# A two-layer decoder trunk: conv taps of one FFN quarter issued a unit later, and two block subtractions written as one

## The chip, the core and the metric

The kernel runs on one core of a Trainium2 chip. The core has five engines that run their own instruction streams in program order and wait for each other through semaphores: PE (TensorE, matmuls; its weight loads are listed as PEld), DVE (VectorE), ACT (ScalarE), POOL (GpSimd) and SP (SyncE, which here only issues DMAs). The metric is the time of one execution on the device in microseconds; less is better. "us" below is microseconds.

## What is computed

Layer 0 is a pooling mixer and a conv FFN, layer 1 an attention over one shared K/V and a conv FFN, each followed by a residual sum and a layer norm. All is in float32, 256 tokens by 2048 features. What the change touches is the conv FFN (hidden width 5504 for the gate and as many for the value):

```python
def conv_ffn(h, w_up, conv_w, conv_b, w_down):
    S = h.shape[1]
    u = h @ w_up
    up = jnp.pad(u, ((0, 0), (CONV_WIDTH - 1, 0), (0, 0)))
    c = conv_b + up[:, 0:S] * conv_w[0]
    for j in range(1, CONV_WIDTH):
        c = c + up[:, j:j + S] * conv_w[j]
    gate, val = jnp.split(c, 2, axis=-1)
    return (jax.nn.silu(gate) * val) @ w_down
```

## The kernel before

**Units.** All matrix products with weights are cut into units, one for each block of up to 512 rows by 512 columns of a weight matrix. `units` lists them in the order in which PE takes them; each entry has the weight block, a function that issues the matmuls, a `post` for the last unit of a group, and, for some blocks of the down-projection, a kind "a" or "b". `run_units` (L126) walks through the list. For unit i it calls `ahead(i)`, which issues loads for up to five units further on and splits for up to three units further on; then it issues the unit's matmuls; then every entry of `pending` that is due; then the `post`. `later(n, fn)` puts a function on `pending` for n units on, and `later(0, fn)` calls it at once. So the list of units and the calls of `later` fix the program order on every engine by hand.

**Splits.** A weight block comes by DMA (SP, L72) into one of three `raw` buffers. ACT rounds it to a high part `wh` (L82) and DVE subtracts to get the low part `wl` (L83); each has four buffers. A product of two such numbers takes three matmuls: high by high, low by high, high by low. A load waits until the raw buffer of three loads ago was split, and a split waits until PE has left the buffer of four units ago.

**Blocks with seven products.** For many blocks of the down-projection the 2 x 2 block product is done with seven products in place of eight (Strassen's scheme in Winograd's form). There the weight block is split twice: kind "a" takes three of the four quadrants as they are, kind "b" the sums of quadrants. `split_sums` (L90) makes both. With r11 and r12 the left and right halves of the upper rows (`B1`) and r21, r22 those of the lower rows (`B2`), kind "a" casts the left half and r22 on ACT (L103), then issues on DVE the difference r12 - r11 (L104), the two low parts (L106), and three differences, each written over its input (L107 to L109). Kind "b", one unit later, casts the right half and then the left half on ACT (L96) and subtracts for the low parts (L97). There are 46 such pairs. The sums on the activation side are made in `left_sums` (L625); its third sum (L647) is the one that multiplies the left upper quadrant of kind "b".

**The FFN.** `ffn(lay)` (L548) takes the hidden width in quarters q0 to q10 of 512 (q10 has 384). `up(q, ...)` puts four units for the gate half and four for the value half; between them stand groups of the down-projection of earlier quarters. A group is one block of 512 output columns (`c`). When the value half of a quarter has run, `val_post` calls `val_chain` (L665): `evac` copies the sums out of the accumulators (L577 on ACT, L578 on DVE), then `conv` issues the three taps (L586 and L591 on ACT, L592 on DVE), `valued` multiplies with the gate (L670), and `three` splits the product into `gq[q]`, tile `g` (L287 on ACT, L283 on DVE), which the down-projection reads as left operand. When `conv` is issued is set by the last line of `val_chain` through `done`, `after` and `at`: `done` has an entry for q4 and q7 alone; for all others the default counts, which is the unit that has just run, plus 0 or 1. With `quick` (q10 alone) the second and third tap are issued together with the first, otherwise one and two units later. `three` is issued at least one unit after `valued`.

**The last stretch.** In layer 1 the value half of q10 is the last of the up-projection. Behind it stand the groups of the last part of the down-projection over q8, q9 and q10. Blocks of q9 have seven products in column blocks 0 and 2. `turns` (L452) puts the first unit of column block 1 ahead of the last one of column block 0, so that the order is: q8 of block 0, q9 of block 0 (a, then b), q8 of block 1, q10 of block 0, q9 of block 1, q10 of block 1, and so on. The matmuls of q8 and q10 are those of `go_t` (L235 to L237), those of q9 with seven products L224 to L226. The first unit that reads q10's `g` is the fifth behind the up-projection.

Of the kernel before, what the change touches and what calls it, by code (L numbers as in the profile page):

```python
# [13 lines left out]
OP = mybir.AluOpType  # L14
# [4 lines left out]
P = 128  # L19
NQ = 4  # L20
FF = 5504
NF = FF // P
# [10 lines left out]
def trunk(ctx: ExitStack, tc: tile.TileContext, x, pool_w_in, pool_w_grp, pool_scale, pool_w_out,  # L33
# [3 lines left out]
    V, A, PE = nc.vector, nc.scalar, nc.tensor  # L37
# [15 lines left out]
    state = {"loaded": 0, "split": 0, "done": 0}  # L53
# [34 lines left out]
    B1, B2, N1, N2 = slice(0, 2), slice(2, 4), slice(0, 256), slice(256, 512)  # L88

    def split_sums(i, kind):  # L90
        h = wh[i] = wp.tile([P, 4, 512], F32R, name=f"wh{i}", tag="wh")
        l = wl[i] = wp.tile([P, 4, 512], F32R, name=f"wl{i}", tag="wl")
        if kind == "b":
            r = raw.pop(i - 1)
            for n in (N2, N1):
                A.copy(h[:, :, n], r[:, :, n])  # L96
                V.tensor_tensor(l[:, :, n], r[:, :, n], h[:, :, n].bitcast(F32), OP.subtract)  # L97
            return
        r = raw[i]
        r11, r12, r21, r22 = r[:, B1, N1], r[:, B1, N2], r[:, B2, N1], r[:, B2, N2]  # L100
        parts = [(slice(0, 4), N1), (B2, N2)]
        for k, n in parts:
            A.copy(h[:, k, n], r[:, k, n])  # L103
        V.tensor_tensor(r12, r12, r11, OP.subtract)  # L104
        for k, n in parts:
            V.tensor_tensor(l[:, k, n], r[:, k, n], h[:, k, n].bitcast(F32), OP.subtract)  # L106
        V.tensor_tensor(r22, r22, r12, OP.subtract)  # L107
        V.tensor_tensor(r21, r21, r22, OP.subtract)
        V.tensor_tensor(r11, r22, r11, OP.subtract)  # L109

    def ahead(i):
        while state["loaded"] < min(len(units), i + LD_AHEAD + 1):
# [7 lines left out]
    def later(n, fn):  # L120
        if n == 0:
            fn()
        else:
            pending.append([n, fn])
# [154 lines left out]
    def quad_tile(nm):  # L279
        return xcp.tile([P, 4, 2, XW], F32R, name=nm, tag="xc")  # L280
# [4 lines left out]
    def split_act(dst, src):  # L285
        n = src.shape[1]
        A.copy(dst[:, 0:n, 0, :T], src)  # L287
        lo_part(dst, src, n)
# [237 lines left out]
    def add_grp(g):  # L526
# [12 lines left out]
             True, 0, 0, after=lambda q: to_tokens(q))  # L539
# [8 lines left out]
    def ffn(lay):  # L548
# [9 lines left out]
        free, done = {}, {}  # L558
# [6 lines left out]
        def evac(ps, nb, mode):  # L565
            fp = pools["ffn"]
            u = pads()

            def tmp():
                return fp.tile([P, T], F32, name="ut", tag="t1", bufs=4)  # L570

            if mode == "x":
                norm_evac(ps, nb, tmp, lambda m: u[:, m, 2:])
                return u
            for m in range(nb):
                t = tmp()
                A.copy(t, ps[m][:, T:])  # L577
                V.tensor_tensor(u[:, m, 2:], ps[m][:, :T], t, OP.add)  # L578
            return u

        def conv(u, blk0, nb, then, quick=False):
            cv = cvec[lay]
            c = pools["ffn"].tile([P, 4, T], F32, name="c", tag="t4")
            for m in range(nb):
                j = blk0 + m
                A.activation(c[:, m, :], u[:, m, 2:], AF.Identity, scale=cv[:, 2, j:j + 1], bias=cv[:, 3, j:j + 1])  # L586

            def tap(i, to):
                for m in range(nb):
                    j = blk0 + m  # L590
                    A.activation(to[:, m, :], u[:, m, i:i + T], AF.Copy, scale=cv[:, i, j:j + 1])  # L591
                V.tensor_tensor(c[:, :nb], c[:, :nb], to[:, :nb], OP.add)  # L592

            def second():
                tap(1, pools["ffn"].tile([P, 4, T], F32, name="a", tag="t4"))

            def third():
                tap(0, u[:, :, 0:T])
                then(c)

            for n, fn in ((1, second), (2, third)):
                later(0 if quick else n, fn)
# [22 lines left out]
        def left_sums(q, s):  # L625
            pool, tag = (hp, "h") if q in (2, 5, 7) else (lnp, "sq")
            two = pool.tile([P, 2, 2, 2, P], F32R, name="xs01", tag=tag)

            def apart():
                return [lnp.tile([P, 2, P], F32R, name=f"xs3{nm}", tag=nm) for nm in ("S", "Q")]  # L630

            if q in (2, 5, 7):
                one = apart()
            else:
                one = pools["ffn"].tile([P, 2, 2, P], F32R, name="xs2", tag="xs", bufs=1)
                one = [one[:, 0], one[:, 1]]
            if len(sevens[q]) < 4:
                own = apart()
            else:
                own = [gq[q][:, 0:2, hl, P:T] for hl in range(2)]  # L640
            xs[q] = [[two[:, i, hl] for hl in range(2)] for i in range(2)] + [one, own]
            a11, a12, a21, a22 = (s[:, k:k + 2, t * P:t * P + P] for k, t in ((0, 0), (2, 0), (0, 1), (2, 1)))
            f = pools["ffn"].tile([P, 4, 2 + T], F32, name="f", tag="t4")[:, :, :T]
            d = [f[:, i].rearrange("p (k t) -> p k t", k=2) for i in range(4)]
            V.tensor_tensor(d[0], a21, a22, OP.add)
            V.tensor_tensor(d[1], d[0], a11, OP.subtract)
            V.tensor_tensor(d[2], a11, a21, OP.subtract)  # L647
            V.tensor_tensor(d[3], a12, d[1], OP.subtract)  # L648

            def rest():  # L650
                both = f[:, 0:2].rearrange("p s (k t) -> p s k t", k=2)
                vs = [((two[:, :, 0], two[:, :, 1]), both), (xs[q][2], d[2]), (xs[q][3], d[3])]
                for v, src in vs:
                    A.copy(v[0], src)
                for v, src in vs:
                    V.tensor_tensor(v[1], src, v[0].bitcast(F32), OP.subtract)  # L656

            later(1, rest)

        def val_post(q, nb, mode):  # L660
            def post(ps):
                later(1 if q == 0 else 0, lambda: val_chain(q, nb, mode, ps))
            return post

        def val_chain(q, nb, mode, ps):  # L665
            u = evac(ps, nb, mode)

            def valued(c):
                s = gates.pop(q)
                V.tensor_tensor(s[:, :nb], s[:, :nb], c[:, :nb], OP.mult)  # L670

                def three():
                    gq[q] = quad_tile("g")
                    split_act(gq[q], s[:, :nb])
                    if q in sevens:
                        left_sums(q, s)

                at(free.get(q, 0), three)

            after(done.get(q, state["done"] + (0 if q in (2, 5, 10) else 1)), lambda: conv(u, NF + 4 * q, nb, valued, q == 10))  # L680

        def after(u, fn):
            later(max(u - state["done"], 0), fn)

        def at(u, fn):
            later(max(u - state["done"], 1), fn)
# [13 lines left out]
        def down(n, last):  # L700
            qs = order[chunks[n][0]]
            rows = [(512 * q, min(512, FF - 512 * q)) for q in qs]
            srcs = [lambda q=q: gq[q] for q in qs]
            groups = []
            mark = len(units)
            for c in range(4):
                sv = {j: (lambda q=q: xs[q]) for j, q in enumerate(qs) if c in sevens.get(q, ())}
                group_tm(w_dn, rows, 512 * c, 512, srcs, tm_post(lay, n, c), apart=last and c == 3,
                         seven=sv, early=early_post(c, not last))
                groups.append(units[mark:])  # L710
                del units[mark:]
            return groups
# [3 lines left out]
        for n in (0, 1):  # L716
            d = down(n, False)
            q = chunks[n + 1][0]
# [5 lines left out]
        d = down(2, False)  # L724
# [19 lines left out]
    def to_tokens(q):  # L744
        if q == 0:
            ST["hb"] = hp.tile([P, 4, T], F32, name="hb", tag="h")
        hb = ST["hb"]
        hf = hb.rearrange("p m t -> p (m t)")
        V.transpose(hf.rearrange("p (t m c) -> p m t c", t=2, m=4), H[q].rearrange("p m (t c) -> p m t c", t=2))

        def to():
            HT[q] = hp.tile([P, 4, T], F32, name="ht", tag="h").rearrange("p a t -> p (a t)").rearrange(
                "p (t c) -> p t c", t=2)
            return HT[q].rearrange("p t c -> p (t c)")

        moves(hf, to)
# [314 lines left out]
    with tc.tile_pool(name="pool", bufs=1) as pp:  # L1071
# [5 lines left out]
        for l in range(2):  # L1077
            n = 80 if l == 0 else 64
            r = pp.tile([80, P], F32, name=f"vrow{l}")
# [92 lines left out]
```

## Time and profile before

| | |
|---|---|
| median of 3 runs | 2040.58 us (2040.13 to 2041.29) |
| the profiled execution | 2042.79 us, of which the span of the trace is 2041.0 us |
| mean granted TensorE clock | 0.998 |
| DMA | 405.88 MB, 199 GB/s over the span |
| DVE groups that the edits touch | L107, L108, L109: 46 each, 692, 692 and 684 ns of one |

A row of the order of time gives start, duration, engine, line of the kernel, operation, output tile <- input tiles, shapes and count; in brackets stands how long the engine had been idle before it, and what released it. A row of the list of waits reads: who waited <- for whom: us in total, times, longest. A row of the busy times in a stretch gives the stretch, its length, the busy time of PE, PEld, DVE, ACT and POOL with the number of instructions, the granted TensorE clock as a share of full speed, the busy share of the DMA engines and GB/s. A row of groups gives the count, then busy us and mean ns of one, then the idle time before them. Durations of matmuls overlap: what one costs in a stream is the step from one start to the next.

### The profile page before, as it was taken

To read this page: it belongs to the slowest core of one execution; us is meant where nothing else is said; L and a number is where in the kernel's file an instruction comes from. 1 tells how busy PE (TensorE), PEld (TensorE's weight loads), DVE (VectorE), ACT (ScalarE), POOL (GpSimd) and SP (SyncE) were. 2 spreads that over 40 slices of the span, in tenths; PEclk is the share of its full clock that TensorE was granted. 3 is DMA by queue.
4 is the path that set the end of the run, shared out by engine and by line. 5 is a ranking of instruction groups with operands and counts; after the bars stand their busy time and mean duration, and the time that the engine had idled before them with its cause. 6 is when DMAs were issued, how large, how long until landed. Compare 5 with 4: busy or idle time off the path is not lost. (4 is left out here: it accounts for less than half of the span.)

```text
span 2041.0 us, 30664 instructions
## 1 busy us (share of the span) xinstructions
PE 2029.8 (99%) x12316; PEld 1805.3 (88%) x12316; DVE 1648.8 (81%) x1973; ACT 1235.0 (61%) x1634; POOL 75.2 (4%) x112
## 2 busy tenths in 40 slices
PE   9999999999999999999999999999999999999999
PEld 8898988889889888889888888998898889889987
DVE  6859877988998888889755667787888878889998
ACT  5544686656766575657444344587765666567662
POOL 2000000000000001100000000000001000000100
PEclk9999999999999999999999999999999999999999
DMA  8655567656665667865556555557667646765764
GB/s 255 208 202 189 166 209 212 189 195 215 205 194 189 219 211 199 239 217 162 187 193 202 176 170 176 178 188 224 185 187 230 223 147 227 216 196 177 221 209 167
DMA packets 278302, 405.88 MB, mean 199 GB/s; under 512 B 80414, under 2 KB 95668, under 8 KB 277904
## 3 DMA queue, kind: packets, MB, share of 16 engines
q1 hardware_dynamic: 266144, 389.72, 58.4%
q0 software_dynamic: 11584, 13.55, 4.4%
q8 instruction: 96, 1.57, 0.3%
q10 hardware_dynamic: 432, 0.66, 0.1%
q14 instruction: 46, 0.38, 0.1%
HBM read 380.01 MB, written 2.10 MB: 187 GB/s over the span
## 5 line engine op out<-in xcount | busy, mean ns | idle before, releaser
L165 PE MATMUL acc<-xc,wh 128*128 128x512 f32 x3264 | 1150.3, 396 | 0.0
L166 PE MATMUL acc<-xc,wl 128*128 128x256 f32 x3264 | 915.9, 281 | 0.4 <-DVE wl L83 0.4
L83 DVE TENSOR_TENSOR wl<-raw,wh 128x2048 fp32r<-128x2048 f32 (+2 forms) x330 | 713.8, 2171 | 238.8 <-ACT wh L82 233.0
L82 ACT CAST wh<-raw 128x2048 fp32r<-128x2048 f32 (+2 forms) x330 | 596.5, 1814 | 279.7 <-PE acc L165 136.5
L165 PEld LDWEIGHTS acc<-xc,wh 128*128 128x128 f32 x3264 | 615.9, 189 | 144.7 <-DVE o L1024 0.6
L166 PEld LDWEIGHTS acc<-xc,wl 128*128 128x128 f32 x3264 | 615.4, 189 | 0.9 <-DVE wl L83 0.7
L96 ACT CAST wh<-raw 128x1024 fp32r<-128x1024 f32 x92 | 93.3, 1050 | 146.5 <-PE acc L165 69.4
L97 DVE TENSOR_TENSOR wl<-raw,wh 128x1024 fp32r<-128x1024 f32 x92 | 108.8, 1219 | 38.6 <-ACT wh L96 38.5
L103 ACT CAST wh<-raw 128x1024 fp32r<-128x1024 f32 x92 | 72.2, 834 | 49.8 <-PE acc L165 42.9
L586 ACT ACTIVATE c<-u,cv 128x256 f32<-128x256 f32 x172 | 89.6, 593 | 12.5 <-DVE f L648 8.2
L577 ACT COPY ut<-acc 128x256 f32<-128x256 f32 x164 | 56.3, 371 | 67.4 <-PE acc L166 67.2
L236 PE MATMUL t<-wl,g 128*128 128x512 f32 (+1 forms) x243 | 93.9, 387 | 1.9 <-DVE wl L83 1.9
L235 PE MATMUL t<-wh,g 128*128 128x512 f32 (+1 forms) x243 | 94.6, 389 | 0.8 <-ACT wh L82 0.8
L237 PE MATMUL t<-wh,g 128*128 128x512 f32 (+1 forms) x243 | 94.0, 387 | 0.0
L268 POOL DMA_DIRECT2D ht<-w x24 | 20.3, 848 | 1842.9 <-DVE ht L817 1106.6
L106 DVE TENSOR_TENSOR wl<-raw,wh 128x1024 fp32r<-128x1024 f32 x92 | 83.7, 951 | 0.2 <-ACT wh L103 0.2
L591 ACT ACTIVATE a<-u,cv 128x256 f32<-128x256 f32 x172 | 73.4, 498 | 7.0 <-DVE g L656 7.0
L578 DVE TENSOR_TENSOR u<-acc,ut 128x256 f32<-128x256 f32 x164 | 60.2, 414 | 21.0 <-ACT ut L577 21.0
L225 PE MATMUL t<-wl,g 128*128 128x256 f32 x272 | 76.4, 281 | 0.0
L224 PE MATMUL t<-wh,g 128*128 128x256 f32 x272 | 76.4, 281 | 0.0
L226 PE MATMUL t<-wh,g 128*128 128x256 f32 x272 | 76.3, 281 | 0.0
L591 ACT ACTIVATE u<-u,cv 128x256 f32<-128x256 f32 x172 | 73.4, 499 | 0.0
(274 smaller groups left out, 3398.1 us busy)
## 6 DMA issues: line engine op xcount, KB each, us to landing
raw<-in_ffn_w_up_dram SPq DMA_DIRECT2D x160, 1024.0 KB, 5.1
raw<-in_ffn_w_down_dram SPq DMA_DIRECT2D x80, 1024.0 KB, 5.2
raw<-in_pool_w_out_dram SPq DMA_DIRECT2D x16, 1024.0 KB, 5.0
raw<-in_shared_w_k_dram SPq DMA_DIRECT2D x16, 1024.0 KB, 5.0
raw<-in_attn_w_q_dram SPq DMA_DIRECT2D x16, 1024.0 KB, 5.2
raw<-in_shared_w_v_dram SPq DMA_DIRECT2D x16, 1024.0 KB, 5.3
raw<-in_attn_w_o_dram SPq DMA_DIRECT2D x16, 1024.0 KB, 5.0
raw<-in_pool_w_in_dram SPq DMA_DIRECT2D x12, 1024.0 KB, 5.5
```

Source lines behind the costliest of these rows:

```text
L82: A.copy(wh[i][:, s], r[:, s])
L83: V.tensor_tensor(wl[i][:, s], r[:, s], wh[i][:, s].bitcast(F32), OP.subtract)
L96: A.copy(h[:, :, n], r[:, :, n])
L97: V.tensor_tensor(l[:, :, n], r[:, :, n], h[:, :, n].bitcast(F32), OP.subtract)
L106: V.tensor_tensor(l[:, k, n], r[:, k, n], h[:, k, n].bitcast(F32), OP.subtract)
L165: PE.matmul(ps[m], h[:, k, c], q[:, k, :, :T], start=st, stop=False)
L166: PE.matmul(ps[m][:, :T], l[:, k, c], q[:, k, 0, :T], start=False, stop=sp and not shifted)
L235: PE.matmul(to, xh, h[:, k, c], start=j == 0 and k == 0, stop=False)
L236: PE.matmul(to, xh, l[:, k, c], start=False, stop=False)
L237: PE.matmul(to, xl, h[:, k, c], start=False, stop=j == len(r0s) - 1 and k == nk - 1)
L586: A.activation(c[:, m, :], u[:, m, 2:], AF.Identity, scale=cv[:, 2, j:j + 1], bias=cv[:, 3, j:j + 1])
L591: A.activation(to[:, m, :], u[:, m, i:i + T], AF.Copy, scale=cv[:, i, j:j + 1])
```

## The change

Two things are edited. In `split_sums`, the two last differences of kind "a" (r21 - r22 and r22 - r11) become one subtraction over the left half of all four row blocks, with r22 repeated for both; the second result thereby changes its sign (r11 - r22), and the third sum in `left_sums` changes its sign with it (a21 - a11), so that their product is the same. In `val_chain`, the unit at which `conv` is issued stays as it was in layer 0, and for q10 in layer 1 it is one unit later.

```diff
-        r11, r12, r21, r22 = r[:, B1, N1], r[:, B1, N2], r[:, B2, N1], r[:, B2, N2]
+        r11, r12, r22 = r[:, B1, N1], r[:, B1, N2], r[:, B2, N2]
...
         V.tensor_tensor(r22, r22, r12, OP.subtract)
-        V.tensor_tensor(r21, r21, r22, OP.subtract)
-        V.tensor_tensor(r11, r22, r11, OP.subtract)
+        both = r[:, :, N1].rearrange("p (b k) n -> p b k n", b=2)
+        V.tensor_tensor(both, both, r22.unsqueeze(1).to_broadcast([P, 2, 2, 256]), OP.subtract)
...
             V.tensor_tensor(d[1], d[0], a11, OP.subtract)
-            V.tensor_tensor(d[2], a11, a21, OP.subtract)
+            V.tensor_tensor(d[2], a21, a11, OP.subtract)
             V.tensor_tensor(d[3], a12, d[1], OP.subtract)
...
-            after(done.get(q, state["done"] + (0 if q in (2, 5, 10) else 1)), lambda: conv(u, NF + 4 * q, nb, valued, q == 10))
+            after(done.get(q, state["done"] + (0 if q in (2, 5) or (q == 10 and lay == 0) else 1)), lambda: conv(u, NF + 4 * q, nb, valued, q == 10))
```

## The prediction

> **What bounds the kernel.** I read the shares of the page first, then the list of waits of PE over the whole span, then the order of instructions around the only long wait.
>
> ```profile
> span 2041.0 us, 30664 instructions
> PE 2029.8 (99%) x12316; PEld 1805.3 (88%) x12316; DVE 1648.8 (81%) x1973; ACT 1235.0 (61%) x1634; POOL 75.2 (4%) x112
> PE t L236 <- DVE wl L83: 1.9, 1, 1.9
> ...
> PE acc L166 <- DVE wl L83: 0.4, 1, 0.4
> ```
>
> PE works for 2029.8 of 2041.0 us, and the work left to it is the same after the change. So a gain can only come from PE's waits, and a faster DVE is worth nothing by itself. The longest wait in PE's list is the one at L236 (once, 1.9 us). In order of time it lies in the second FFN, 60 us before the end, with one at L235 just ahead of it:
>
> ```profile
> 1976.78 0.28 PE L226 MATMUL s<-wh,xs 128*128 128x256 f32 x1
> 1977.88 0.50 PE L235 MATMUL t<-wh,g 128*128 128x512 f32 x1 [0.83 <-ACT wh L82]
> 1980.27 0.50 PE L236 MATMUL t<-wl,g 128*128 128x512 f32 x1 [1.89 <-DVE wl L83]
> ...
> 1984.72 0.40 PE L236 MATMUL t<-wl,g 128*128 128x512 f32 x1
> ...
> 1987.28 0.40 PE L235 MATMUL t<-wh,g 128*128 128x512 f32 x1
> 1980.50:1984.50 4.00, 4.00 (x12) 3.12 (x12) 4.00 (x3) 1.83 (x2) 0.00 (x0) 0.57 0.73 234
> ```
>
> I call the last unit of the up-projection (value half of quarter q10) U0, and those behind it, in the order in which the last down-projection and `turns` lay them out, U1 (q8, column block 0), U2 and U3 (q9, kinds a and b), U4 (q8, block 1), U5 (q10, block 0), U6 (q9, block 1). The rows show U4: 24 matmuls of 512 columns from 1977.88 on, U5 begins at 1987.28. At full speed a matmul takes (1987.28 - 1984.72) / 11 = 0.233 us. U3's last one begins at 1976.78 and is half as wide (0.12), so U4 could have begun at 1976.90 and ended 24 x 0.233 = 5.59 us later, at 1982.49. It ends 4.79 us after that: 0.98 us until the first matmul, 2.16 us until the second, and 1.65 us because the granted clock is 0.57 in the window behind the wait (last row, third number from the end). The two waits thus cost more than their 2.7 us.
>
> What U4 waits for is seen on DVE and ACT:
>
> ```profile
> 1968.03 0.69 DVE L108 TENSOR_TENSOR raw<-raw 128x512 f32<-128x512 f32 x1
> 1968.64 0.68 DVE L109 TENSOR_TENSOR raw<-raw 128x512 f32<-128x512 f32 x1
> 1969.24 2.43 DVE L97 TENSOR_TENSOR wl<-raw,wh 128x1024 fp32r<-128x1024 f32 x2
> ...
> 1971.93 0.74 DVE L578 TENSOR_TENSOR u<-acc,ut 128x256 f32<-128x256 f32 x2
> 1974.87 0.96 DVE L592 TENSOR_TENSOR c<-c,a 128x768 f32<-128x768 f32 x1 [2.19 <-ACT a L591]
> 1976.07 0.96 DVE L592 TENSOR_TENSOR c<-c,u 128x768 f32<-128x768 f32 x1 [0.24 <-ACT u L591]
> 1977.06 0.96 DVE L670 TENSOR_TENSOR c<-c 128x768 f32<-128x768 f32 x1
> 1977.93 2.28 DVE L83 TENSOR_TENSOR wl<-raw,wh 128x2048 fp32r<-128x2048 f32 x1
> 1980.14 0.95 DVE L283 TENSOR_TENSOR g<-c,g 128x768 fp32r<-128x768 f32 x1
> 1981.01 1.75 DVE L83 TENSOR_TENSOR wl<-raw,wh 128x1536 fp32r<-128x1536 f32 x1
> 1968.10 1.05 ACT L96 CAST wh<-raw 128x1024 fp32r<-128x1024 f32 x1 [7.57 <-DVE raw L107]
> ...
> 1970.31 0.91 ACT L577 COPY ut<-acc 128x256 f32<-128x256 f32 x3
> 1972.05 1.59 ACT L586 ACTIVATE c<-u,cv 128x256 f32<-128x256 f32 x3 [0.82 <-DVE u L578]
> ...
> 1975.94 1.89 ACT L82 CAST wh<-raw 128x2048 fp32r<-128x2048 f32 x1
> 1978.05 0.83 ACT L287 CAST g<-c 128x768 fp32r<-128x768 f32 x1 [0.22 <-DVE c L670]
> ```
>
> U4's cast (1975.94) and subtraction (1977.93) stand behind the conv of q10: nine ACT instructions from 1972.05 to 1975.94, two DVE sums and one product to 1977.9, with DVE idle for 2.19 us in between. The order is that of the code: U0's `post` issues the conv before the unit that follows issues U4's split.
>
> **The change, part by part.** *Conv of q10 in the second FFN.* Nothing is added or removed; conv and product move behind the split of U4, and q10's gate value g behind the split of U5. ACT: the copies L577 end at 1971.22. U4's raw block is there, since its load left at 1961.48 and the DMA share is 0.02 from 1970 on; its buffer is free, since PE left U0 at 1966.35.
>
> ```profile
> 1961.48 0.37 SPq L72 DMA_DIRECT2D raw<-in_ffn_w_down_dram  x1
> 1970.00:1972.00 2.00, 2.00 (x11) 1.60 (x10) 2.00 (x5) 1.22 (x4) 0.00 (x0) 1.00 0.02 9
> 1966.35 0.40 PE L235 MATMUL t<-wh,g 128*128 128x512 f32 x1
> ```
>
> So the cast runs 1971.2 + 1.89 = 1973.1 and the subtraction 1973.1 + 2.28 = 1975.4, as DVE is free from 1972.67. PE wants the high part at 1976.90 and the low part at 1977.13: 1.7 us to spare, and the whole 4.79 us fall away.
>
> What comes late instead is g. The conv starts on ACT at 1973.1, 1.05 us later than before. Its first sum on DVE came 2.82 us after its start, its second 4.02, the product 5.01: now 1975.9, 1977.1 and 1978.1, the product done at 1979.1. U5's split: the cast is issued behind the nine instructions, at 1973.1 + 3.89 = 1977.0, and is done before the product; subtraction 1979.1 + 1.75 = 1980.85. Then g, whose cast waits for the product: 1979.2 + 0.83 = 1980.0, low part 1980.85 + 0.95 = 1981.8. U5 now starts at 1982.49 and reads g's low part in its third matmul, at 1982.95: 1.15 us to spare. U6's split is queued behind g on both engines: cast 1980.0 + 1.9 = 1981.9, subtraction to 1984.2; wanted at 1982.49 + 18 x 0.233 = 1986.7. SP's queue isn't passed by anything: its loads keep their order, and the one that waits for U4's raw buffer can leave at 1975.4, where the old subtraction of U4 ended at 1977.93 + 2.28 = 1980.2. So this edit is -4.79 us. If the cover of 1.15 us at U5 were gone, each us beyond it would cost one us, and up to 1.65 for the clock.
>
> *One subtraction for two*, 46 times. L108 and L109 occupy 1968.03 to 1969.24, 1.21 us from start to start. The fused one has 1024 elements and an operand that is repeated; the nearest row is L413, which also writes over its input and repeats an operand.
>
> ```profile
> L413 DVE TENSOR_TENSOR h<-h,rm 128x1024 f32<-128x1024 f32 x12 | 14.6, 1217 | 0.0
> ```
>
> 1.22 us, of which about 0.08 overlap the next instruction, as L108's 0.69 does against its step of 0.61: 1.14, a saving of 0.07 us (bounds -0.01, if nothing overlaps, and 0.15, by the three durations; I take the step, as the two rows in question show it), 46 x 0.07 = 3 us of DVE that is not on the path. PE sees it only at the wait of 0.4 us at L166, behind a stretch with two such pairs: 0.1 us (bounds 0 and 0.3, two pairs at 0.15). [...] The reversed sign in L647 costs the same instruction.
>
> Sum: -4.79 - 0.1 = -4.9 us. The profiled execution took 2042.79 us, 1.79 outside the span; the median of the runs shown is 2.21 lower, so 2040.58 - 4.9 = **2035.7 us**, span 2036.1.
>
> **The rivals.** *The clock doesn't fall without the profiler, or not by that much* (only 0.98 + 2.16 us come back). For it: the profiled execution is 2.21 us above the median, more than the clock's 1.65. Against it: the three runs lie within 1.16 us, so they don't mix runs with and without it. Time: 2040.58 - 3.14 - 0.1 = 2037.3. [...]
>
> *The wait moves to U5*, with g's low part behind U6's split as well: 1984.2 + 0.95 = 1985.15 against 1982.95, so 2.2 us, and 1.65 for the clock; 3.85 of 4.9 are given back: 2039.5. For it: the two engines have 1.15 us to spare there at most, on an estimate that chains ten instructions. Against it: in the code g comes before U6's split on both engines.
>
> *Slower: the fused write holds up ACT's cast of the right half.* Today this cast begins after L107 (row 1968.10), while L108 and L109 still run. If it had to wait for the fused write too, it would begin at 1969.35, and DVE at its subtraction at 1970.45 instead of 1969.24: 1.2 us for each pair, 2.4 for a stretch of two. Most stretches hide 2.2 us, like the one at 392.81 (low part ready 388.32 + 2.29 = 390.61); at 1890.51 only 0.40 are hidden, and nothing at the wait of L166.
>
> ```profile
> 388.32 2.29 DVE L83 TENSOR_TENSOR wl<-raw,wh 128x2048 fp32r<-128x2048 f32 x1 [0.57 <-ACT wh L82]
> 392.81 0.28 PE L166 MATMUL acc<-xc,wl 128*128 128x256 f32 x1
> 1887.82 2.29 DVE L83 TENSOR_TENSOR wl<-raw,wh 128x2048 fp32r<-128x2048 f32 x1 [1.30 <-ACT wh L82]
> 1890.51 0.28 PE L166 MATMUL acc<-xc,wl 128*128 128x256 f32 x1
> ```
>
> That makes 2.4 + 2.0, twice 1.65 for the clock, and some 2 us for stretches that go 0.2 over: 9.7 - 4.8 = +4.9, or 2045.5; it outweighs the gain once a pair loses over about 0.8 us. Against it: the fused write covers the same columns as the two did, and the cast didn't wait for those.
>
> *It doesn't do what it says*: the delay by a unit would fall away only if q10 had an entry of its own in `done`; it has none (4 and 7 have). What is left is that U4 waits for something that these rows don't show, and then only the 0.1 us remain: 2040.5.
>
> **How the numbers follow.** Forecast 0.62 (its own range 2034.6 to 2036.8, from the bounds of both terms and 0.6 us of scatter), clock rival 0.18, U5 0.07, slower 0.06, nothing moved 0.07. A measurement of this kernel tells about 0.2%, 4.1 us, from no change: the border is 2036.5. Nearly all of the forecast and a little of the clock rival lie below it: faster 0.60. Slower over 2044.7: the third rival and a little of what I don't see, 0.08; within, 0.32. The range 2034.2 to 2039.5 holds the first three and leaves out about 0.17.
>
> **What would show it.** Right: no PE wait at U4, granted clock 1.00 around 1980, U4's cast ahead of the nine conv instructions on ACT, g's low part done at least 1 us before U5's third matmul, a fused instruction of 1.22 us, and the last 50 us of the trace shifted by 4.8 us as a whole. Wrong: a wait at U5 with releaser L283; a cast L96 released by the fused line; a wait later among the q9 units of columns 2, where loads now set the pace; or a median within 3.2 us of the old one though the waits are gone.

## The result, and the profile after

The changed kernel takes 2036.49 us (median of 13 runs, 2035.59 to 2036.94) against 2040.91 us for the kernel before in the same comparison (13 runs, 2039.27 to 2043.64): 4.4 us less, a ratio of 0.9977 with a 95% interval of 0.9969 to 0.9985. The forecast was 2035.7. The gain in the trace's span is larger than in the time: over the runs with a span on record the median span is 2034.3 us in the changed kernel (13 runs) and 2039.2 and 2039.1 in the kernel before (32 and 26 runs of the experiments below), so 4.9 or 4.8 us less. The rest of a run, outside the span, went the other way, from 1.8 to 2.1 us; the section on the prediction comes back to it.

The order of time of PE around U4 in the changed kernel (columns as in the rows of before):

```profile
1974.37 0.28 PE L226 MATMUL s<-wh,xs 128*128 128x256 f32 x1
1974.49 0.39 PE L235 MATMUL t<-wh,g 128*128 128x512 f32 x1
1974.72 0.40 PE L236 MATMUL t<-wl,g 128*128 128x512 f32 x1
...
1980.06 0.40 PE L235 MATMUL t<-wh,g 128*128 128x512 f32 x1
1980.30 0.40 PE L236 MATMUL t<-wl,g 128*128 128x512 f32 x1
1980.53 0.40 PE L237 MATMUL t<-wh,g 128*128 128x512 f32 x1
```

U3's last matmul, U4's first and second follow each other in steps of 0.12 and 0.23 us. U5 begins at 1980.06, which is 5.57 us after U4's start; in the kernel before, counted from 1976.90, where U4 could have begun, it was 1987.28 - 1976.90 = 10.38. So 4.8 us are gone from U4. What made room, on DVE and ACT of the same kernel:

```profile
1970.39 2.29 DVE L83 TENSOR_TENSOR wl<-raw,wh 128x2048 fp32r<-128x2048 f32 x1 [0.38 <-ACT wh L82]
1973.06 0.96 DVE L592 TENSOR_TENSOR c<-c,a 128x768 f32<-128x768 f32 x1 [0.38 <-ACT a L591]
...
1976.13 1.75 DVE L83 TENSOR_TENSOR wl<-raw,wh 128x1536 fp32r<-128x1536 f32 x1
1977.80 0.95 DVE L283 TENSOR_TENSOR g<-c,g 128x768 fp32r<-128x768 f32 x1
1968.43 1.92 ACT L82 CAST wh<-raw 128x2048 fp32r<-128x2048 f32 x1
1970.25 1.58 ACT L586 ACTIVATE c<-u,cv 128x256 f32<-128x256 f32 x3
```

The cast and the subtraction of U4 (2048 elements) now come before the conv. The subtraction ends at 1972.68 and is wanted at 1974.72. g's low part ends at 1978.75 and is wanted by U5's third matmul at 1980.53. DVE's idle time before the first sum L592 has gone from 2.19 to 0.38 us: the same instructions, in an order in which one engine's work covers the other's.

The list of PE's waits and the shares of the page after:

```profile
span 2034.0 us, 30619 instructions
PE 2026.6 (100%) x12316; PEld 1802.8 (89%) x12316; DVE 1645.9 (81%) x1927; ACT 1234.3 (61%) x1634; POOL 75.2 (4%) x112
PE xT L516 <- DMA xin<-in_x_dram: 1.6, 1, 1.6
PE warm L1057 <- DVE one L1053: 1.1, 1, 1.1
PE acc L166 <- DVE wl L83: 0.3, 1, 0.3
```

L235 and L236 are no longer in it, and L166 fell from 0.4 to 0.3. The span of the profiled execution fell by 7.0 us, more than the medians. The other 2.2 us lie in the first 15 us, where the two profiled executions differ in code that the change doesn't touch. In the kernel before, PE waited there for 1.8 us at L168 until 10.08, and between 10 and 15 us the granted clock was 0.66. In the changed kernel that wait is missing (PE waited 1.6 us earlier, for its input), and the clock was 1.00. First the kernel before, then the changed one (the wait; then stretch, length, busy times, clock, DMA share, GB/s):

```profile
PE acc L168 <- ACT wh L82: 1.8, 1, 1.8
10.00:15.00 5.00, 4.70 (x24) 4.49 (x25) 2.73 (x4) 2.30 (x5) 0.00 (x0) 0.66 1.05 360
```

```profile
10.00:15.00 5.00, 4.97 (x42) 4.90 (x43) 3.73 (x6) 3.62 (x8) 0.00 (x0) 1.00 1.03 380
```

### The profile page after: what moved, and what is told of

It reads as the page before. It is cut to its first block, busy times and chain, and to the rows that moved or that the text cites. A ratio compares the mean times of both kernels' runs of the same rounds, so it can differ in the third digit from the quotient of the medians.

```text
span 2034.0 us, 30619 instructions
## 1 busy us (share of the span) xinstructions
PE 2026.6 (100%) x12316; PEld 1802.8 (89%) x12316; DVE 1645.9 (81%) x1927; ACT 1234.3 (61%) x1634; POOL 75.2 (4%) x112
## 4 chain that ended last, share of the span: by engine, by line
PE 99%; DVE 1%; DMA 0%; ACT 0%; SPq 0%; issue 0%; DVEq 0%
PE acc L165 43%; PE acc L166 22%; PE t L235 4%; PE t L237 4%; PE t L236 4%; PE acc L169 3%; PE acc L170 3%; PE acc L168 3%; PE s L224 2%; PE s L226 2%; PE s L225 2%; PE t L226 2%; PE t L225 2%; PE t L224 2%; PE s L954 0%; PE o L1021 0%
## 5 line engine op out<-in xcount | busy, mean ns | idle before, releaser
L165 PE MATMUL acc<-xc,wh 128*128 128x512 f32 x3264 | 1150.2, 396 | 0.0
L166 PE MATMUL acc<-xc,wl 128*128 128x256 f32 x3264 | 915.9, 281 | 0.3 <-DVE wl L83 0.3
L165 PEld LDWEIGHTS acc<-xc,wh 128*128 128x128 f32 x3264 | 615.9, 189 | 144.6 <-DVE o L1024 0.6
L166 PEld LDWEIGHTS acc<-xc,wl 128*128 128x128 f32 x3264 | 615.4, 189 | 0.7 <-DVE wl L83 0.6
L96 ACT CAST wh<-raw 128x1024 fp32r<-128x1024 f32 x92 | 93.3, 1050 | 147.1 <-PE acc L165 71.4
L97 DVE TENSOR_TENSOR wl<-raw,wh 128x1024 fp32r<-128x1024 f32 x92 | 108.7, 1221 | 41.4 <-ACT wh L96 41.3
L235 PE MATMUL t<-wh,g 128*128 128x512 f32 (+1 forms) x243 | 93.9, 386 | 0.0
L236 PE MATMUL t<-wl,g 128*128 128x512 f32 (+1 forms) x243 | 93.1, 383 | 0.0
L225 PE MATMUL t<-wl,g 128*128 128x256 f32 x272 | 76.4, 281 | 0.0
L224 PE MATMUL t<-wh,g 128*128 128x256 f32 x272 | 76.3, 281 | 0.0
```

Source lines behind the costliest of these rows:

```text
L165: PE.matmul(ps[m], h[:, k, c], q[:, k, :, :T], start=st, stop=False)
L166: PE.matmul(ps[m][:, :T], l[:, k, c], q[:, k, 0, :T], start=False, stop=sp and not shifted)
L224: PE.matmul(to, xh, h[:, k, n], start=opens and kk == 0, stop=False)
L225: PE.matmul(to, xh, l[:, k, n], start=False, stop=False)
L235: PE.matmul(to, xh, h[:, k, c], start=j == 0 and k == 0, stop=False)
L236: PE.matmul(to, xh, l[:, k, c], start=False, stop=False)
```

## The experiments

Each was compared with the kernel before on the same chip. A comparison with the changed kernel's 2036.49 us is one between comparisons; the medians of the kernel before in them (2040.91, 2040.95 and 2040.79 us) agree within 0.2 us. The theory was the prediction's: PE waited at U4 for a split that stood behind q10's conv; the wait and the slower clock behind it are the whole gain; the fused subtraction counts only where DVE is late. The rivals were a gain from the lighter DVE, a clock that falls for another cause, and a new wait at U5.

**One part alone: the conv.**

```diff
-... (0 if q in (2, 5, 10) else 1) ...
+... (0 if q in (2, 5) or (q == 10 and lay == 0) else 1) ...
```

> The kernel before with only the conv of q10 a unit later in the second FFN; three subtractions stay three. Theory (the gain is the wait at U4): no wait of PE at U4, granted clock 1.00 around it, U5's first matmul 24 x 0.233 us behind U4's first, and 4.8 us less than before (2036.1 against 2040.9). Rival (the fused subtraction carries a good part of the gain by making DVE faster along the whole kernel): the wait at U4 is smaller but not gone, and less than 3 us come back. In the list of waits the one of 0.4 us at L166 stays as it was by both.

Measured: 2036.70 against 2040.95 us, ratio 0.9978 (0.9970 to 0.9987), 4.25 us less. PE's list of waits has nothing at U4; the wait at L166 is still there:

```profile
PE acc L166 <- DVE wl L83: 0.6, 1, 0.6
```

In the profile U5 follows U4's start by 5.57 us, as in the changed kernel. The conv alone gives the gain, within what a timing can tell.

**The other part alone: the subtraction.** The reverse of the edit above, on the changed kernel.

> The kernel before with only the fused subtraction (and the sign that goes with it); the conv of q10 stays where it was. Theory: the waits of PE at U4 stay (0.8 and 1.9 us, less 0.1), the clock still falls to half for about one window behind them, the wait at L166 goes from 0.4 to about 0.3 us, and the time falls by 0.1 to 0.3 us, which a timing cannot tell from nothing. Rival (DVE's saved 3 us count): 2 to 3 us faster. Rival (the fused write holds up ACT's cast): slower by 4 us or more, with casts L96 released by the fused line.

Measured: 2042.74 us, ratio 1.0006 (0.9997 to 1.0014): no change that can be told. The median is 1.8 us above the 2040.95 of the kernel before, because 7 of these 11 runs have a mean clock of 0.998 or less, against 6 of the 32; why so many is not known. At equal mean clock, 0.999, the medians are 2040.68 us (4 runs) and 2040.85 (25 runs). The waits and the low clock at U4 are those of before:

```profile
1977.69 0.50 PE L235 MATMUL t<-wh,g 128*128 128x512 f32 x1 [0.61 <-ACT wh L82]
1980.09 0.49 PE L236 MATMUL t<-wl,g 128*128 128x512 f32 x1 [1.89 <-DVE wl L83]
1858.03 0.39 PE L166 MATMUL acc<-xc,wl 128*128 128x256 f32 x1 [0.36 <-DVE wl L83]
1980.50:1984.50 4.00, 4.00 (x12) 3.13 (x11) 4.00 (x3) 1.67 (x3) 0.00 (x0) 0.57 0.81 235
```

DVE is busy for 1646.1 us in place of 1648.8, so 2.7 us less, and PE doesn't notice but for 0.06 us at L166 and 0.2 at L235. The rival that DVE's saved time counts has fallen. So has the one that the fused write holds up ACT: its casts waited for the fused line in 3 of 46 pairs, 0.5 us in all, and each time it was the cast of the left half, which reads what that line writes. In the kernel before, the left half's cast waited for L109 in 9 pairs, 1.9 us in all. The cast of the right half, which the rival was about, waited for it in none.

**The clock by itself.** Matmuls whose result is cleared by U4's first one keep PE busy where it waited:

```diff
+                if j == 0 and not apart and r0s[0][0] == 4096 and c0 == 512:
+                    q = xqs[0]()
+                    for i in range(12):
+                        PE.matmul(ps[0], ones4, q[:, i % 4, :, :T], start=True, stop=True)
                 held.append((h, l, xqs[j]()))
```

> The kernel before, with twelve matmuls of 512 columns more ahead of U4's first matmul; they read q8's g, are there on time, write to U4's own accumulator, and what they leave is cleared by U4's first matmul. PE is thus busy for 12 x 0.233 = 2.8 us in the stretch in which it waited. Theory (the clock falls because PE paused there, and that costs 1.65 us by itself): U4's low part still comes at the same time, so a wait of about 0.6 us at L236 is left, but the matmuls behind it step at 0.233 us, granted clock 1.00, and U5 begins 1.6 us earlier than in the kernel before when both are set against the start of U3; the time falls by 1.6 us though work was added. Rival (the clock falls for another reason, such as the load of the stretch): the steps stay at 0.43 us for about 3.4 us and the time is that of before or longer.

```profile
1975.38 2.99 PE L248 MATMUL t<-g,ones 128*128 128x512 f32 x12
1978.20 0.39 PE L235 MATMUL t<-wh,g 128*128 128x512 f32 x1
1978.80 0.49 PE L236 MATMUL t<-wl,g 128*128 128x512 f32 x1 [0.21 <-DVE wl L83]
1979.13 0.39 PE L237 MATMUL t<-wh,g 128*128 128x512 f32 x1
1979.37 0.40 PE L235 MATMUL t<-wh,g 128*128 128x512 f32 x1
1980.50:1984.50 4.00, 4.00 (x19) 3.21 (x18) 3.91 (x5) 1.73 (x3) 0.00 (x0) 1.00 0.93 324
```

In the profiled execution it went as expected: twelve matmuls more, the wait shrunk to 0.21 us, steps of 0.23 behind it, granted clock 1.00 where it was 0.57. The medians, 2040.37 against 2040.95 (ratio 0.9998, 0.9989 to 1.0007), don't show the 1.6 us. The mean granted clock of each run says why: 5 of 11 runs have 1.000 and 6 have 0.999, where one window like that of the kernel before (the 3.4 us from 1980.8 to 1984.2, behind its pause at U4, with steps of 0.43 us and a granted clock of 0.52) makes, as an estimate, 1 - 3.4 x 0.48 / 2040 = 0.999. By that only some of the executions kept the clock, and the five lie 1.3 us below the six (medians 2039.78 and 2041.07). A second form left no pause at all, with fourteen matmuls that read g on both sides:

```diff
-                    for i in range(12):
-                        PE.matmul(ps[0], ones4, q[:, i % 4, :, :T], start=True, stop=True)
+                    for i in range(14):
+                        PE.matmul(ps[0], q[:, i % 4, 0, :P], q[:, i % 4, :, :T], start=True, stop=True)
```

> The kernel before with fourteen matmuls more ahead of U4, now with q8's g as both operands, 14 x 0.233 = 3.3 us, so that no pause is left at all. With twelve, and a constant as one operand, 5 of 11 runs kept a mean clock of 1.000, where 1 of 32 did so in the kernel before. [...] Rival (the clock follows from DVE's and ACT's load there): 0.999 as before, and 0.2 us slower than before.

```profile
1973.73 3.38 PE L248 MATMUL t<-g 128*128 128x512 f32 x14
1976.95 0.40 PE L235 MATMUL t<-wh,g 128*128 128x512 f32 x1
1977.18 0.39 PE L236 MATMUL t<-wl,g 128*128 128x512 f32 x1
```

10 of 11 runs now have a mean clock of 1.000, and the median is 2039.71 against 2040.79: 1.1 us less (ratio 0.9993, 0.9984 to 1.0002), though 3.3 us of work were added. The time's interval reaches to nothing, so the time alone doesn't settle it; the clock of the runs does. Mean granted clocks of all runs:

| kernel | pauses of PE at U4 | runs | of these at 1.000 |
|---|---|---|---|
| before | 0.98 and 2.16 us | 32 and 26 | 1 and 4 |
| subtraction alone | 0.8 and 2.2 us | 11 | 0 |
| twelve matmuls more | 0.4 us | 11 | 5 |
| fourteen matmuls more | none | 11 | 10 |
| conv alone | none | 11 | 9 |
| changed kernel | none | 13 | 12 |

Only the profiled execution of each kernel shows where its pauses lie; the mean clocks of all the others fit them: the kernel before has one below 1.000 in 53 of 58 runs, not in the profiled one alone, and the kernels without a pause at U4 in 4 of 35. Whether the six of the twelve matmuls' runs that have 0.999 owe it to the rest of the pause or to the constant operand was not told apart: the second form changed both.

**One unit too many, two units too many.** The number of units by which q10's conv is put off, in the changed kernel:

```diff
-... (0 if q in (2, 5) or (q == 10 and lay == 0) else 1) ...
+... (0 if q in (2, 5) or (q == 10 and lay == 0) else 2 if q == 10 else 1) ...
```

> The changed kernel with the conv of q10 two units later in place of one (behind the splits of U4 and U5, so that g comes behind the split of U6). Theory (what is late next is g at U5, by the order on DVE and ACT): the conv begins on ACT 1.5 us later than in the changed kernel, g's low part ends about 2.1 us later, and PE waits for L283 at the third matmul of U5 for 0.5 to 0.8 us; a pause that short leaves the clock at 1.00, so the time rises by that alone and is 2037 to 2037.5. Rival (a pause of any length halves the clock for a window): 1.65 us more, 2038.5 to 2039. Rival (there is enough slack for a second unit): no wait, same time as the changed kernel.

```profile
1979.61 0.95 DVE L283 TENSOR_TENSOR g<-c,g 128x768 fp32r<-128x768 f32 x1
1980.10 0.40 PE L236 MATMUL t<-wl,g 128*128 128x512 f32 x1
1980.62 0.50 PE L237 MATMUL t<-wh,g 128*128 128x512 f32 x1
```

Measured: 2036.54 us (9 runs), the same as the changed kernel's 2036.49. g's low part ends at 1980.56, and U5's third matmul, due at 1980.33, which is 0.23 us after the second, begins at 1980.62: 0.3 us late. The place is as expected. The size is about a half of it, and the time is below the 2037 to 2037.5 that was expected. The clock stayed: 8 of 9 runs have 1.000. With `3 if q == 10`:

> The changed kernel with the conv of q10 three units later (behind the split of U6, the group's own sums, and g behind the split of U7). Theory (the room ends at two units): the first sum on DVE begins near 1979, g's high part is done about 3.3 us after U5 wants it and its low part some 4 us after that; PE waits 5 to 8 us at U5 and the clock falls behind it, so 2042 to 2046: all of the gain is lost. Rival (loads and engines have room, since two units later cost 0.4 us): 2037 to 2038.

```profile
PE t L237 <- DVE g L283: 3.4, 1, 3.4
PE t L235 <- ACT g L287: 2.6, 1, 2.6
```

Measured: 2045.86 us, ratio 1.0024 (1.0014 to 1.0033), 9.4 us above the changed kernel and 5 above the kernel before. PE waits 2.6 us for g's high part and, two matmuls later, 3.4 us for its low part; the clock is at half behind the first of them and stays there past the second (0.50 from 1983.5 to 1993.5), and all 9 runs have 0.997 or 0.998. What is late next is g, as the prediction had it, and the room for it is a little less than two units.

**The slower rival's price.** Kind "b" casts the left half first, so that ACT has to wait for the fused line:

```diff
-            for n in (N2, N1):
+            for n in (N1, N2):
```

> The changed kernel with the two halves of kind b in the other order: ACT casts the left half first, which has to wait for the fused subtraction, where the right half could be cast while it ran. This puts the price of the slower rival on the chip. Theory (the stretches with two pairs hide about 2.2 us, except those before 1855, 1890 and 1949, which hide 0, 0.4 and 1.2): DVE loses 1.1 to 1.2 us for each of the 46 pairs, PE waits 2.3 us in place of 0.3 at 1855, 1.9 at 1890 and about 1 at 1949, elsewhere less than 0.2 each, and the clock falls behind one or two of these: 5 to 10 us slower than the changed kernel, 2041.5 to 2046.5. Rival (81% busy DVE has room enough): under 1 us slower.

```profile
PE gb L888 <- DVE dg L886: 2.1, 1, 2.1
PE s L225 <- DVE wl L97: 1.9, 2, 1.1
PE acc L166 <- DVE wl L83: 1.6, 2, 1.4
PE s L224 <- ACT wh L96: 1.3, 1, 1.3
```

Measured: 2048.24 us (4 runs, 2045.36 to 2049.68), ratio 1.0038 (1.0023 to 1.0054): 11.7 us above the changed kernel, more than the 5 to 10 expected; between the profiled executions it is 2043.2 - 2034.0 = 9.2. The order of the two casts is worth more than the whole change. The theory holds as to the part of the kernel where DVE has no room: the waits shown lie behind 1850, in the last stretches of the second FFN and at its end. But the places are only partly those expected. Near 1855, where 2.3 us were expected, PE waited 0.8 us at L225 and 0.2 at L166; at 1890 it was 1.4 for 1.9; at 1949 it was 2.3 for about 1; and the 2.1 us at L888, at the end, were not expected. About half of the waiting is inside the pairs (L224 and L225, which read kind "b" itself), not at the unit behind. The price was not paid by every pair either: DVE's waits for L96 rose from 41.3 to 47.3 us in all, 6 us, where 46 pairs at 1.1 would have made 50. Elsewhere ACT reached these casts late anyhow: in the changed kernel it waited at L96 for PE 35 times, 108 us in all.

**The remaining wait.** The wait at L166 looks like U4's: ACT's first tap for q8 ahead of the cast of the next unit. In the changed kernel:

```diff
+... else 2 if q == 8 and lay == 1 else 1) ...
```

> The changed kernel with the conv of q8 in the second FFN one more unit later (its value is needed only in the last part of the down-projection). The wait of PE at L166 at 1855 stands behind that conv as U4 stood behind that of q10: ACT ran the first tap ahead of the cast of the next unit. Theory: the cast comes 1.5 to 2 us earlier, the wait of 0.3 to 0.6 us is gone, no new one comes, 2036.1, which a timing can hardly tell from 2036.5. Rival (the conv then collides with the next units' splits): the wait comes back one or two units later, 0.3 us or more.

```profile
1855.63 0.28 PE L166 MATMUL acc<-xc,wl 128*128 128x256 f32 x1
1888.99 0.38 PE L166 MATMUL acc<-xc,wl 128*128 128x256 f32 x1 [0.80 <-DVE wl L83]
```

The wait near 1855 is gone, and one of 0.80 us stands at 1888.99, at the end of the next group, where the prediction had found 0.40 us to spare. So a new wait did come, as the rival had it, though some 33 us later and not one or two units; what made DVE late there was not followed up. 2037.35 us (ratio 0.9985, 0.9976 to 0.9995) isn't faster than the changed kernel. No kernel of the study is faster than the changed one.

## Why the prediction held, point by point

- **U4, -4.79 us: right.** The profile shows -4.8 at that place, and the conv alone measured -4.25 with an interval of -2.7 to -6.1 us. U4's low part was 2.0 us early (1.7 predicted).
- **The clock's share, 1.65 us: right, and the rival without it wrong.** The time alone can't tell them apart: 2036.49 lies halfway between 2035.7 and the rival's 2037.3. What decides is that U5 begins 4.8 us earlier, not 3.1, that the mean clock rose to 1.000 in 12 of 13 runs, and that matmuls put into the pause raised it too. That rival's support was that the profiled execution lay 2.21 us above the median. This has another cause: that execution had lost a second window at the start of the kernel (0.66 between 10 and 15 us; the profiled execution of the subtraction alone has the same 0.66 there and a mean clock of 0.998, too). 6 of the 32 runs of the kernel before have that mean clock, at 2042.3 to 2042.8 us. The argument against the rival, three runs within 1.16 us, was weak: the 58 later runs do mix five that kept the clock, 44 with a mean of 0.999 and nine with 0.998. The forecast took its sum from the profile but its base from the median, which was right; its span of 2036.1 was 2.1 us too high for the same reason.
- **The only long wait: misread.** The list of PE's waits before has a second one of 1.8 us, at L168 near 10 us, in rows that the prediction leaves out. The change doesn't touch it, and it differs between profiled executions (1.7 us with the subtraction alone, 1.2 with the conv alone, none in the changed kernel), so the sum is not affected. It stands just ahead of the second slow window of that profile.
- **g at U5: right as to what is late next, 0.6 us too cautious.** 1.78 us to spare in place of 1.15; putting the conv off once more used this up and 0.3 us beyond, and a third time cost 9 us.
- **The fused subtraction: right as to the instruction; what it does to the time is not settled.** It takes 1.225 us where 1.22 was read off L413. DVE's busy time fell by 2.9 us (3 predicted). Its worth to PE is below what a timing shows: the wait at L166 went from 0.42 to 0.27 in the changed kernel and to 0.36 with the subtraction alone, while it stood at 0.60 with the conv alone, so it scatters by as much as was predicted for it. The runs show two more effects, which largely cancel: at equal mean clock the median span is about 0.55 us shorter with the fused line (2038.55 against 2039.1 us for the subtraction alone, 2034.25 against 2034.8 for the changed kernel and the conv alone), and the time outside the span is longer. It is 2.1 to 2.2 us in all 56 runs of the kernels with the fused line and 1.7 to 1.9 in all 91 of those without it. The prediction kept it at 1.79, and its term of 0.1 us has neither effect; why the time outside the span rose is open.
- **ACT held up by the fused write: wrong, as expected.** 2 casts waited for the fused line, 0.4 us in all. Its price of 9.7 us is near the 9.2 between the profiled executions with the casts swapped and below the 11.7 of the medians; the places were partly wrong.
- **The sum, -4.9 us, against -4.4 measured** (interval 3.1 to 6.3) in the comparison: right, and the spans of the runs have 4.8 to 4.9. The time came out 0.8 us above the forecast: the base was 0.3 higher (2040.91 for 2040.58), and of the 0.5 that the gain is short, the time outside the span makes 0.3 to 0.4. The interval leaves out no gain at all, but not the border of 4.1 us below which the prediction calls a change too small to tell. The runs of the kernel before scatter by 4 us, and with their mean clock: of the 32, the one with 1.000 took 2039.17 us, and the medians of those with 0.999 and 0.998 are 2040.85 and 2042.55; the sum can't be resolved better by timing.

## What to carry to other kernels

Where one engine is 99% busy, go to its few waits and read what stands ahead of the late instruction in the order of the other engines; here, moving independent work behind it cost nothing as long as the moved work's own reader had room (1.78 us at U5), and that room should be worked out on both engines before the step is made larger. Price a pause of TensorE by the start of the next unit, not by the wait that the list shows: here 2.7 us of listed waits cost 4.8.

## What the runs showed of the hardware

In the kernel before, a pause of PE of 3.1 us with one matmul in its middle was followed by one window of 3.4 us at a granted clock of 0.52 (steps of 0.43 in place of 0.23 us from 1980.8 to 1984.2) in the profiled execution, and 53 of its 58 later runs have a mean clock below 1.000. Fourteen matmuls without use in the same place kept it at 1.000 in 10 of 11 runs. With the conv three units later, a single pause of 2.7 us came ahead of the slower clock: PE's last matmul before it began at 1980.29, the next at 1983.25, and the clock behind it was 0.50.

```profile
1980.29 0.40 PE L237 MATMUL t<-wh,g 128*128 128x512 f32 x1
1983.25 0.58 PE L235 MATMUL t<-wh,g 128*128 128x512 f32 x1 [2.56 <-ACT g L287]
1983.50:1993.50 10.00, 6.56 (x16) 4.61 (x16) 7.75 (x9) 1.50 (x1) 0.00 (x0) 0.50 0.51 159
```

Shorter pauses were not always followed by it: with the casts swapped, the clock was 1.00 from 1885 to 1895, a stretch that has PE's wait of 1.4 us in it. Behind the wait of 0.80 us at 1888.99 with q8's conv put off, L165 and L166 together take 0.35 us, no more than near 1856 in the same trace, and the mean clock is 1.000 in 8 of 10 runs. With the conv two units later a matmul that came 0.3 us late left it at 1.000 in 8 of 9 runs. Where the limit lies was not measured.
